# Sliding-window attention with sinks: one merged block of 128 visible logits in place of two masked blocks

## The chip, the cores and the metric

The kernel runs on one core of one Trainium2 chip. The metric is device time in microseconds, measured as the median of several executions; one further execution is recorded by the hardware profiler. Engines are named as in the profile: PE is TensorE (PEld its weight loads), DVE VectorE, ACT ScalarE, POOL GpSimd, SP the engine that issues most transfers.

## The reference, cut to what matters

Two decoder layers on 2048 tokens of width 1024, float32. Layer A (forgetting attention) and the shared keys and values are not touched. Layer B is the part in question: 16 query heads in 4 groups share 4 key/value heads of 64 columns; each query sees the 128 keys up to its own, and a learned sink per head takes part in the softmax but brings no value.

```python
logits = jnp.einsum('bnqhgd,bnkhd->bnhgqk', qb, k_band) * scale    # k_band: previous and own block of 128
diff = (jnp.arange(WINDOW)[:, None] + WINDOW) - jnp.arange(2 * WINDOW)[None, :]
in_window = (diff >= 0) & (diff < WINDOW)
...
logits = jnp.where(valid[None, :, None, None], logits, -jnp.inf)
probs = jax.nn.softmax(jnp.concatenate([logits, sink], axis=-1), axis=-1)[..., :-1]
out = jnp.einsum('bnhgqk,bnkhd->bnqhgd', probs, v_band)
...
h = h + (o * jax.nn.silu(gate)) @ w_out_b[j]
```

For query q of a block, key column j of the own block is visible if j <= q, and column j of the previous block if j > q. So exactly one of the two is visible for every j, and 128 in all.

## The kernel before, in words

The sequence is cut into 16 blocks of 128 queries. A unit is one block i and one group g of four heads: 64 units, unit u = 4 i + g. Every float32 product is made of split operands: a high part (rounded for the fast matmul) and a low part (what is left).

`attention_b` (L1239) writes its work as steps. Step n (L1423) holds, in this order:

- **scores(n)** (L1274): for each of four heads two matmuls (L1279, L1282) of 256 key columns into one PSUM tile of two banks; a masked maximum per head on VectorE (L1288), which adds the band mask in PSUM and reduces; small instructions for the negated maximum and the sink (L1294, L1297, L1298); four exponentials with row sums on ScalarE (L1301); sum and reciprocal (L1305, L1306); normalization of all 1024 columns on GpSimd (L1307).
- **weights_t(n - 3)** (L1311): eight transposes of 128 x 128 on TensorE (helper line L347) into a PSUM tile of two banks, then the high part by ScalarE (L1325) and the low part by VectorE (L1326).
- six matmuls of the output projection (L1404), fed from a generator that works eight steps behind.
- **values(n - 4)** (L1329): four matmuls of 512 columns (L1337): two blocks, each by high and low part. Both halves of the value split lie side by side, so ScalarE copies the low half of the result to SBUF (L1344), VectorE adds the halves in two instructions (L1346), GpSimd multiplies by the gate (L1350), ScalarE and VectorE split the result again (L1352, L1353).
- six more projection matmuls. Half a block's projection takes 24 of them in one PSUM bank `pb`; VectorE adds the residual (L1410) and a transfer stores it.

Block 0 has no previous block: its four units work on 128 columns. `load` (L1247) fetches queries and keys of the next block in three transfers and clears part of an operand tile on GpSimd (L1257); `load_v` fetches values and gates. In steps 4 to 11 the output weights are loaded and split (L1386 on ScalarE, L1387 on VectorE, 1024 columns each).

The first eight steps run inside `projections`: the last eight gate tiles of 24 matmuls (L720) each have one attention step ahead of them (the `hook`, L714). From step 8 on projection fills TensorE.

PSUM has eight banks; the layout `BANKS` gives `b2` three tiles of two banks, `pa` and `pb` one each. Scores and transposes draw from `b2`, values from `pa`, projection from `pb`, the gate from `pb` and `b2` in turn.

The order in which the code is written is not the order on each engine. When the program is built, a scheduler fixes the order of each engine's instructions from modelled times, and waits are set by tile; the trace shows the order that came out.

Of the kernel before, what the change touches and what calls it, by code (L numbers as in the profile page):

```python
# [13 lines left out]
F32R = mybir.dt.float32r  # L14
BF16 = mybir.dt.bfloat16
I32 = mybir.dt.int32
AF = mybir.ActivationFunctionType
# [70 lines left out]

BANKS = dict(b2=3, pa=1, pb=1)
BANKS_ATT = dict(sc=3, mx=1, pa=1, pb=1, ac=1)  # L90

# [58 lines left out]
class Trunk:  # L150
# [56 lines left out]
    def constants(self):  # L207
# [30 lines left out]

        self.band = tile_("band", [P, 2, P], BF16)
        nc.gpsimd.memset(self.band, 0.0)  # L240
        select(self.band[:, 0, :], self.band[:, 0, :], [[1, P]], -1, -1, NEG)
        select(self.band[:, 1, :], self.band[:, 1, :], [[-1, P]], 0, 1, NEG)

# [29 lines left out]
        self.gq16 = row("gq16", a["qnorm_b_g"][:, :ROT], ROT)  # L273
        self.nsink = tile_("nsink", [P, H])

# [6 lines left out]
    def vectors(self):  # L282

        nc = self.nc
        self.load_vectors(self.loads[1:])
        for t in (self.g_qb, self.g_kb):
            for s in range(2):
                nc.vector.memset(t[s * HD : s * HD + ROT, :], 1.0)
        nc.vector.tensor_single_scalar(self.nsink, self.sink, -1.0, ALU.mult)

# [331 lines left out]
    def projections(self, normed, groups, row, later=None, pre=None, hook=None, first=None):  # L622
# [75 lines left out]
        for gi, grp in enumerate(groups):  # L698
# [539 lines left out]
    def attention_b(self, w_out, res, dst):  # L1238
# [3 lines left out]
        N = len(units)  # L1242
        blk, st = {}, {}

        def load(i):

            k0 = max(i - 1, 0) * P  # L1247
            w = (i + 1) * P - k0
            ts_ = slice(i * P, (i + 1) * P)
            t = self.sb("big", [P, 4 * 1024], F32R)  # L1250
# [6 lines left out]
            nc.gpsimd.memset(f_(k2[:HD, :, :w]), 0.0)  # L1257
# [16 lines left out]
        def scores(u):  # L1274
            i, g = units[u]
            ka, k2, qa, _, _, w = blk[i]
            ps = self.ps("b2", [P, G, 2 * P])
            for h in range(G):
                nc.tensor.matmul(  # L1279
                    ps[:, h, :w], qa[:, g * G + h, :], ka[:, g, :w], start=True, stop=False  # L1280
                )
                nc.tensor.matmul(  # L1282
                    ps[:, h, :w], qa[:, g * G + h, :], k2[:, g, :w], start=False, stop=True
                )
            mx = self.sb("mx", [P, G], bufs=6)
            mask = self.band.rearrange("p b k -> p (b k)")[:, 2 * P - w :]
            for h in range(G):
                nc.vector.tensor_tensor_reduce(  # L1288
                    out=ps[:, h, :w], in0=ps[:, h, :w], in1=mask, scale=1.0, scalar=NEG,
                    op0=ALU.add, op1=ALU.max, accum_out=mx[:, h : h + 1],  # L1290
                )
            nm, es, rs = (self.sb(x, [P, G], bufs=6) for x in ("nm", "es", "rs"))
            hs = slice(g * G, (g + 1) * G)
            nc.vector.scalar_tensor_tensor(  # L1294
                nm, mx, -(HD**-0.5), self.nsink[:, hs], ALU.mult, ALU.min
            )
            nc.vector.tensor_tensor(es, nm, self.sink[:, hs], ALU.add)  # L1297
            nc.scalar.activation(es, es, AF.Exp)  # L1298
            pf = self.sb("st", [P, G, 2 * P])
            for h in range(G):  # L1300
                nc.scalar.activation(  # L1301
                    pf[:, h, :w], ps[:, h, :w], AF.Exp, bias=nm[:, h : h + 1],
                    scale=HD**-0.5, accum_out=rs[:, h : h + 1],
                )
            nc.vector.tensor_tensor(rs, rs, es, ALU.add)  # L1305
            nc.vector.reciprocal(rs, rs)  # L1306
            nc.gpsimd.tensor_tensor(  # L1307
                pf[:, :, :w], pf[:, :, :w], rs.unsqueeze(2).to_broadcast([P, G, w]), ALU.mult
            )
            st[u] = pf  # L1310

        def weights_t(u):

            i, g = units[u]
            nb = blk[i][5] // P
# [5 lines left out]
            ph, pl = (  # L1321
                php[:, 2 * k + u % 2, :].rearrange("p (b h q) -> p b h q", b=2, h=G)
                for k in range(2)
            )
            nc.scalar.copy(ph[:, :nb], ps[:, :nb])  # L1325
            nc.vector.tensor_tensor(pl[:, :nb], ps[:, :nb], f_(ph[:, :nb]), ALU.subtract)  # L1326
            st[u] = (ph, pl)

        def values(u):  # L1329
            i, g = units[u]  # L1330
            ph, pl = st.pop(u)
            nb = blk[i][5] // P
            pv = self.ps("pa", [P, G, P])
            for b in range(nb):
                v = blk[i - nb + 1 + b][3]
                for n_, src in enumerate((ph, pl)):
                    nc.tensor.matmul(  # L1337
                        pv.rearrange("p h q -> p (h q)"), v[:, g, :],
                        src[:, b].rearrange("p h q -> p (h q)"),
                        start=(b == 0 and n_ == 0), stop=(b == nb - 1 and n_ == 1),  # L1340
                    )
            t = self.sb("wr", [P, 8, P])
            cr, y = t[:HD, :G, :], t[:, G : G + G // 2, :]
            nc.scalar.copy(cr, pv[HD:])  # L1344
            for s in range(2):
                nc.vector.tensor_tensor(  # L1346
                    y[s * HD : (s + 1) * HD], pv[:HD, s::2, :], cr[:, s::2, :], ALU.add
                )
            pr = slice(g * G // 2, (g + 1) * G // 2)
            nc.gpsimd.tensor_tensor(y, y, blk[i][4][:, pr, :], ALU.mult)  # L1350
            yh, yl = (yt(i, k, pr) for k in range(2))
# [38 lines left out]
        load_v(0)  # L1390
        yield

        def project():
# [29 lines left out]
        for n in range(N + V_LAG_B):  # L1423
            if n < N:
                scores(n)
            if n == T_LAG_B:
                php = self.sb("big", [P, 4, 1024], F32R)
            if n == V_LAG_B + NKV:
# [141 lines left out]
```

## Time and profile before

| | |
|---|---|
| runs of the kernel before, us | 2503.91, 2504.49, 2506.16 (median 2504.49) |
| profiled execution, its own time, us | 2501.05 |
| its span in the profile, us | 2499.3 |
| mean granted TensorE clock | 0.998 |
| first and last score matmul of layer B, us from the span's start | 2089.8 and 2459.2 |
| first and last projection matmul (L1404) | 2150.3 and 2495.1 |

The span is cut on the page into shares by engine; since stages differ, the shares of layer B's attention are read from windows between the times in the last two rows. A row of the groups gives the line of the code, the engine, the operation, output and inputs by name, shapes and count, then busy time, mean ns of one, and how long the engine sat idle before it and for whom. A row of the timeline gives start, length, engine, line, and in brackets the idle time before it with its cause. A weight load (PEld) overlaps the matmul before it, so starts of successive weight loads show the pace of TensorE better than lengths of matmuls.

### The profile page before, as it was taken

What the parts mean: (1) busy time and instruction counts of PE and PEld (TensorE: products, weight loads), DVE (VectorE), ACT (ScalarE), POOL (GpSimd) and SP (SyncE); (2) the same over time, 40 slices, a digit from 0 to 9 for tenths busy, and PEclk for the clock granted to TensorE, in tenths of its full rate; (3) what the DMA queues carried; (4) which work ended last, traced back from release to release, by engine and by line L of the source; (5) the groups of instructions that cost most, each with busy time, mean ns of one, the idle gap of its engine ahead of it and who ended that gap; (6) DMA issues with size and microseconds to landing.
All of it is one profiled execution on the core that took longest, in us unless ns stands there. A gap on an engine that the chain in (4) does not pass through costs nothing.

```text
span 2499.3 us, 37273 instructions
## 1 busy us (share of the span) xinstructions
PE 2450.7 (98%) x12256; PEld 2048.9 (82%) x12256; DVE 1798.3 (72%) x4279; ACT 1307.5 (52%) x2553; POOL 920.6 (37%) x611
## 2 busy tenths in 40 slices
PE   8999999999999999999999999999999999899999
PEld 6788899988888887877877778888888888788887
DVE  7656667736888888888888965556666434888885
ACT  5423333414777777777777761145332213677674
POOL 0000000013777777777777752200011001355543
PEclk9999999999999999999999999999999999999999
DMA  5656545687545655565465559965443424665561
GB/s 183 201 160 190 174 147 157 192 273 220 147 144 157 192 147 157 145 198 150 131 193 166 153 168 291 287 214 165 114 127 88 128 97 143 188 170 159 160 170 64
DMA packets 351520, 419.29 MB, mean 168 GB/s; under 512 B 64928, under 2 KB 248256, under 8 KB 345152
## 3 DMA queue, kind: packets, MB, share of 16 engines
q1 hardware_dynamic: 351328, 416.92, 57.3%
q8 instruction: 97, 1.59, 0.3%
q14 instruction: 95, 0.78, 0.1%
HBM read 265.29 MB, written 151.40 MB: 167 GB/s over the span
## 4 chain that ended last, share of the span: by engine, by line
PE 48%; DVE 4%; DMA 2%; ACT 2%; issue 1%; POOL 1%; SPq 0%; POOLq 0%; ACTq 0%; DVEq 0%
PE b L757 9%; PE pb L1404 6%; PE b L1220 5%; PE pa L1025 4%; PE pb L1059 3%; PE pb L720 3%; PE b L720 3%; PE b L347 2%; PE mx L934 2%; PE sc L983 2%; PE pa L1337 2%; PE sc L982 2%; DMA wr<-wg 1%; PE b L1282 1%; PE b L1279 1%
## 5 line engine op out<-in xcount | busy, mean ns | idle before, releaser
L757 PE MATMUL b<-wh,big 128*128 128x512 f32 (+3 forms) x2560 | 769.9, 375 | 8.9 <-ACT wh L484 8.9
L1001 POOL TENSOR_TENSOR big<-st,big 128x1024 fp32r<-128x1024 f32 (+1 forms) x320 | 659.7, 2076 | 273.6 <-ACT big L1000 171.8
L757 PEld LDWEIGHTS b<-wh,big 128*128 128x128 f32 x2560 | 471.4, 188 | 79.3 <-ACT wh L484 10.9
L757 PE MATMUL b<-wl,big 128*128 128x512 f32 (+3 forms) x1280 | 473.7, 370 | 1.7 <-DVE wl L485 1.7
L1010 DVE TENSOR_TENSOR ac<-ac,st 128x512 f32<-128x512 f32 (+3 forms) x576 | 355.0, 616 | 53.2 <-ACT st L997 24.5
L997 ACT ACTIVATE st<-sc 128x512 f32<-128x512 f32 (+1 forms) x512 | 274.9, 584 | 157.6 <-PE sc L983 79.4
L1025 PE MATMUL pa<-big 128*128 128x512 f32 (+3 forms) x1280 | 327.1, 370 | 3.1 <-POOL big L1001 1.0
L1000 ACT CAST big<-st 128x1024 fp32r<-128x1024 f32 (+1 forms) x320 | 295.5, 924 | 8.0
L757 PEld LDWEIGHTS b<-wl,big 128*128 128x128 f32 x1280 | 241.4, 189 | 38.3 <-DVE wl L485 5.8
L1025 PEld LDWEIGHTS pa<-big 128*128 128x128 f32 x1280 | 222.8, 190 | 49.1 <-ACT sq L1033 16.8
L945 DVE CUSTOM_DVE_ANT_0 mx<-mx,rot 128x128 f32<-128x128 f32 (+3 forms) x240 | 210.5, 877 | 39.6 <-PE mx L934 34.5
L493 ACT ACTIVATE sq<-b,r 128x512 f32<-128x512 f32 (+2 forms) x128 | 77.8, 608 | 301.2 <-PE b L757 298.1
L982 PE MATMUL sc<-big 128*128 128x512 f32 (+3 forms) x640 | 231.1, 365 | 1.3 <-DVE st L540 1.1
L983 PE MATMUL sc<-big 67*128 67x512 f32 (+3 forms) x640 | 229.7, 368 | 0.0
L934 PE MATMUL mx<-big 66*128 66x128 f32 (+3 forms) x660 | 192.1, 365 | 10.4 <-DVE mt L945 9.8
L1059 PE MATMUL pb<-wh,wr 128*128 128x512 f32 x488 | 179.4, 399 | 3.7 <-DMA wr<-wg 3.1
L495 DVE TENSOR_REDUCE sm<-sq 128x8 f32<-128x512 f32 (+2 forms) x128 | 74.9, 585 | 138.9 <-ACT sq L493 138.7
L857 POOL MEMSET rot<- 128x1024 bf16 x1 | 1.0, 952 | 421.0 <-PE pb L347 421.0
L934 PEld LDWEIGHTS mx<-big 66*128 66x128 f32 x660 | 113.6, 191 | 50.0 <-DVE mt L945 20.2
L1307 POOL TENSOR_TENSOR st<-st,rs 128x1024 f32<-128x1024 f32 (+1 forms) x64 | 118.0, 1843 | 93.4 <-DVE rs L1306 88.1
L982 PEld LDWEIGHTS sc<-big 128*128 128x128 f32 x640 | 121.7, 190 | 23.2 <-DVE st L540 1.5
L983 PEld LDWEIGHTS sc<-big 67*128 67x128 f32 x640 | 121.7, 190 | 21.2
(258 smaller groups left out, 4349.3 us busy)
## 6 DMA issues: line engine op xcount, KB each, us to landing
wr<-wg SPq DMA_DIRECT2D x62, 512.0 KB
va<-st SPq DMA_DIRECT2D x32, 512.0 KB
ka<-st SPq DMA_DIRECT2D x64, 256.0 KB
ut<-big SPq DMA_DIRECT2D x16, 1024.0 KB
big<-ka SPq DMA_DIRECT2D x16, 1024.0 KB
big<-qa SPq DMA_DIRECT2D x16, 1024.0 KB
qb<-st SPq DMA_DIRECT2D x64, 256.0 KB
big<-qb SPq DMA_DIRECT2D x16, 1024.0 KB
```

The lines of the kernel that those rows point to most:

```text
L720: nc.tensor.matmul(ps, W[k][dt][:, ft * P : (ft + 1) * P], u[ch][:, dt, :], start=(dt == 0 and i == 0), stop=(dt == NDT - 1 and i == 2),)
L757: nc.tensor.matmul(ps[:, :n], u[tb // 4][:, dt, us], W[k][dt], start=(dt == 0 and i == 0), stop=(dt == NDT - 1 and i == 2),)
L934: mm = nc.tensor.matmul(ps[:, b, :wb], qb[:66, i * P : (i + 1) * P], kb[:66, k0 + b * wb : k0 + (b + 1) * wb], start=True, stop=True,)
L945: nc.vector.tensor_tensor_reduce(out=lg, in0=lg, in1=mask, scale=1.0, scalar=NEG, op0=ALU.add, op1=ALU.max, accum_out=f_(o),)
L982: nc.tensor.matmul(o, ka[:, ks], qa[:, qs], start=not (last and n_), stop=False)
L983: nc.tensor.matmul(o, kb[:, ks], qb[:, qs], start=False, stop=not diag)
L997: nc.scalar.activation(pf[:, off : off + w], ps[:, :w], AF.Exp, scale=HD**-0.5)
L1000: nc.scalar.copy(ph[:, :tw], pf[:, :tw])
L1001: nc.gpsimd.tensor_tensor(pl[:, :tw], pf[:, :tw], f_(ph[:, :tw]), ALU.subtract)
L1010: nc.vector.tensor_tensor(a_, a_, pf[:, off : off + w], ALU.add)
L1025: nc.tensor.matmul(pv[:, q0 : q0 + w], v[:, k, :], src[:, off : off + w], start=(p == 0 and n_ == 0 and i == 0), stop=(last and n_ == 1 an ...
L1059: nc.tensor.matmul(ps, w[:, dt // 2 % 2, wk, dt % 2, :], us[dt][uk], start=(dt == 0 and i == 0), stop=(dt == NDT - 1 and i == 2),)
```

## The change

Layer B's attention is rewritten so that each unit carries one block of 128 logits a head.

- The masks: `band[:, 0]` holds the causal mask for block 0, `band[:, 1]` is 1 where the key column is after the query. The factor 1/8 moves from the exponential into the query gain; the negated sinks and their exponential are dropped.
- **scores**: the same matmuls, placed so that own logits lie in the upper 128 columns. A predicated copy puts the previous block's logits over the hidden ones. The sink is copied into the column just ahead; one maximum over 129 columns, and four exponentials of 129 columns whose row sums hold the sink.
- **weights_t**: four transposes into a PSUM tile of one bank (`fl`), high and low part of 512 columns; then GpSimd multiplies both by the lower triangle (1024 columns).
- **differences**, new, once per block from block 1: value differences between own and previous block, split again, on GpSimd with one ScalarE copy.
- **values**: previous values by high and low part of all weights, plus differences by the triangle's part: four matmuls as before. The output stays in the PSUM tile; the gate product moves to VectorE.
- The operand tiles of `load` are two fixed ones, cleared once each. From the second hook on, the layout `BANKS_B` holds; gate tiles then take `pa` in place of `b2`.

```diff
+BANKS_B = dict(b2=2, fl=1, pa=2, pb=1)
...
+        select(self.band[:, 0, :], self.band[:, 0, :], [[-1, P]], 0, 1, NEG)
+        nc.vector.tensor_tensor(self.band[:, 1], self.tri, self.ident, ALU.subtract)
...
+        nc.vector.tensor_single_scalar(self.g_qb, self.g_qb, HD**-0.5, ALU.mult)
...
-                        ps = self.ps(("pb", "b2")[ft % 2], [P, CH])
+                        ps = self.ps(("pb", "pa" if "fl" in self.banks else "b2")[ft % 2], [P, CH])
...
-            for h in range(G):
-                nc.vector.tensor_tensor_reduce(
-                    out=ps[:, h, :w], in0=ps[:, h, :w], in1=mask, scale=1.0, scalar=NEG,
-                    op0=ALU.add, op1=ALU.max, accum_out=mx[:, h : h + 1],
-                )
...
+                m = self.band[:, 1].bitcast(I16).unsqueeze(1).to_broadcast([P, G, P])
+                nc.vector.copy_predicated(lg, m, ps[:, :, :P])
+            nc.vector.tensor_copy(ps[:, :, P - 1], self.sink[:, g * G : (g + 1) * G])
+            lg = ps[:, :, P - 1 :]
+            nm, rs = (self.sb(x, [P, G], bufs=6) for x in ("nm", "rs"))
+            nc.vector.tensor_reduce(nm, lg, AX.X, ALU.max, negate=True)
+            pf = self.sb("st", [P, G, P + 1])
...
             nc.gpsimd.tensor_tensor(
-                pf[:, :, :w], pf[:, :, :w], rs.unsqueeze(2).to_broadcast([P, G, w]), ALU.mult
+                pf, pf, rs.unsqueeze(2).to_broadcast([P, G, P]), ALU.mult
             )
...
-            ps = self.ps("b2", [P, 2, G, P])
-            for b in range(nb):
-                for h in range(G):
-                    self.flip(ps[:, b, h, :], pf[:, h, b * P : (b + 1) * P])
+            ps = self.ps("fl", [P, G, P])
+            for h in range(G):
+                self.flip(ps[:, h, :], pf[:, h])
+            both, own = (php[:, u % 2, k] for k in range(2))
+            ph, pl = (both[:, k] for k in range(2))
+            nc.scalar.copy(ph, ps)
+            nc.vector.tensor_tensor(pl, ps, f_(ph), ALU.subtract)
+            if i:
+                tri = self.tri.unsqueeze(1).to_broadcast([P, 2 * G, P])
+                nc.gpsimd.tensor_tensor(
+                    own.rearrange("p k h q -> p (k h) q"),
+                    f_(both).rearrange("p k h q -> p (k h) q"), tri, ALU.mult,
+                )
...
+        def differences(i):
+            v, before = f_(blk[i][3]), f_(blk[i - 1][3])
+            t = self.sb("wl", [P, NKV, P])
+            nc.gpsimd.tensor_tensor(t, v, before, ALU.subtract)
+            t_ = t[:, :, :HD]
+            nc.gpsimd.tensor_tensor(t_, t_, t[:, :, HD:], ALU.add)
+            dv = self.sb("wh", [P, NKV, P], F32R)
+            nc.scalar.copy(dv[:, :, :HD], t_)
+            nc.gpsimd.tensor_tensor(dv[:, :, HD:], t_, f_(dv[:, :, :HD]), ALU.subtract)
+            dvs[i] = dv
...
+                terms = ((v, ph), (v, pl), (dv, oh), (dv, ol))
...
+            y = pv[:, 1::2, :]
+            for s in (1, 0):
...
-            nc.gpsimd.tensor_tensor(y, y, blk[i][4][:, pr, :], ALU.mult)
+            nc.vector.tensor_tensor(y, y, blk[i][4][:, pr, :], ALU.mult)
...
+            if n % NKV == 1 and NKV < n < N:
+                differences(n // NKV)
```

More of the change, by code (lines that the diff above doesn't have):

```diff
@@ L1249, in load @@
             ts_ = slice(i * P, (i + 1) * P)
-            t = self.sb("big", [P, 4 * 1024], F32R)
+            if i < 2:
+                operands[i] = self.sb("big", [P, 4 * 1024], F32R)
+            t = operands[i % 2]
             qa = t[:, : H * P].rearrange("p (h q) -> p h q", q=P)
@@ L1292, in scores @@
[L1292 to L1299, printed above, removed]
+                for j, k in enumerate((ka, k2)):
+                    nc.tensor.matmul(
+                        ps[:, h, 2 * P - w :], qa[:, g * G + h, :], k[:, g, :w],
+                        start=j == 0, stop=j == 1,
+                    )
@@ new lines, in weights_t @@
+            st[u] = (ph, pl, own[:, 0], own[:, 1])
+        def differences(i):
[8 more added lines that the diff above has]
+            dvs[i] = dv
@@ L1342, in values @@
-            t = self.sb("wr", [P, 8, P])
-            cr, y = t[:HD, :G, :], t[:, G : G + G // 2, :]
+            ph, pl, oh, ol = st.pop(u)
+            if i:
+                v, dv = blk[i - 1][3], dvs[i]
+                terms = ((v, ph), (v, pl), (dv, oh), (dv, ol))
+            else:
+                v = blk[i][3]
+                terms = ((v, ph), (v, pl))
+            pv = self.ps("pa", [P, G, P])
+            for n_, (v, src) in enumerate(terms):
+                nc.tensor.matmul(
+                    pv.rearrange("p h q -> p (h q)"), v[:, g, :],
+                    src.rearrange("p h q -> p (h q)"),
+                    start=n_ == 0, stop=n_ == len(terms) - 1,
+                )
@@ L1426, in attention_b @@
             if n == T_LAG_B:
[L1427 removed]
+                php = self.sb("big", [P, 2, 2, 2, G, P], F32R)
             if n == V_LAG_B + NKV:
```

53 lines of the change are left out of this document (16 added, 37 removed).

## The prediction

> **What bounds the kernel now.** I read the page's busy times first, then the stretches of the timeline by windows to find the stage, then one step of it instruction by instruction.
>
> ```profile
> span 2499.3 us, 37273 instructions
> PE 2450.7 (98%) x12256; PEld 2048.9 (82%) x12256; DVE 1798.3 (72%) x4279; ACT 1307.5 (52%) x2553; POOL 920.6 (37%) x611
> ```
> ```profile
> core 0: us, PE busy (x) PEld busy (x) DVE busy (x) ACT busy (x) POOL busy (x), PEclk, DMA share, GB/s
> 2125.00:2135.00 10.00, 8.16 (x43) 6.82 (x42) 8.53 (x24) 5.50 (x16) 2.64 (x3) 1.00 0.65 183
> 2145.00:2155.00 10.00, 9.13 (x52) 7.73 (x50) 8.93 (x23) 5.31 (x14) 2.64 (x2) 1.00 0.55 165
> 2165.00:2175.00 10.00, 5.78 (x32) 4.38 (x30) 8.71 (x26) 7.12 (x23) 4.26 (x4) 1.00 0.89 262
> 2250.00:2300.00 50.00, 50.00 (x293) 43.76 (x292) 44.48 (x152) 35.78 (x111) 25.62 (x21) 1.00 0.56 155
> ```
>
> In the settled part of layer B's attention (2250 to 2300) TensorE is never idle and its clock is full; VectorE is at 89%, ScalarE at 72%, GpSimd at 51%. Before that, while the output weights are being split, TensorE loses 1.84, 0.87 and 4.22 us in three stretches. A busy row alone doesn't prove a bound, so here is one step, the weight loads of TensorE in order:
>
> ```profile
> 2300.05 1.23 PEld L1404 LDWEIGHTS pb<-big 128*128 128x128 f32 x6
> 2301.32 0.88 PEld L1337 LDWEIGHTS pa<-big,qn 128*128 128x128 f32 x4
> 2302.24 1.32 PEld L1404 LDWEIGHTS pb<-big 128*128 128x128 f32 x6
> 2303.61 0.19 PEld L1279 LDWEIGHTS b<-big 128*128 128x128 f32 x1
> 2304.68 0.90 PEld L347 LDWEIGHTS b<-ident,st 128*128 128x128 f32 x8
> 2305.55 1.22 PEld L1404 LDWEIGHTS pb<-big 128*128 128x128 f32 x6
> ```
>
> Start to start: six projection matmuls 1.27 us (P), four value matmuls 0.92 (V), six more 1.37 (P), eight score matmuls 1.07 (S), eight transposes 0.87 (F); the step is 5.50 us and nothing in it waits. A transpose thus costs 0.87 / 8 = 0.109 us of TensorE's own time. What TensorE issues per unit sets the period.
>
> **The change part by part.** Durations for the other engines come from these groups (window from 2000 to 2500, shapes apart; the last line from the page):
>
> ```profile
> L1288 DVE CUSTOM_DVE_ANT_0 b<-b,band 128x256 f32<-128x256 f32 x240 | 102.0, 425 | 21.3 <-PE b L1282 16.7
> L1288 DVE DVE_READ_ACCUMULATOR2_ANT mx<- 128x1 f32 x256 | 34.4, 134 | 0.6
> L1297 DVE TENSOR_TENSOR es<-nm,sink 128x4 f32<-128x4 f32 x64 | 10.8, 169 | 2.1
> L1325 ACT CAST big<-b 128x512 fp32r<-128x512 f32 x4 | 2.4, 588 | 0.0
> L1326 DVE TENSOR_TENSOR big<-b,big 128x1024 fp32r<-128x1024 f32 x60 | 73.2, 1220 | 2.2 <-ACT big L1325 2.1
> L1326 DVE TENSOR_TENSOR big<-b,big 128x512 fp32r<-128x512 f32 x4 | 2.7, 682 | 0.0
> L1346 DVE TENSOR_TENSOR wr<-pa,wr 64x256 f32<-64x256 f32 x128 | 52.9, 414 | 3.1 <-ACT wr L1344 2.0
> L1353 DVE TENSOR_TENSOR big<-wr,big 128x256 fp32r<-128x256 f32 x32 | 13.6, 426 | 4.6 <-ACT big L1352 1.6
> L1387 DVE TENSOR_TENSOR big<-wr,big 128x1024 fp32r<-128x1024 f32 x8 | 16.0, 1998 | 0.0
> L1410 DVE TENSOR_TENSOR sq<-pb,sq 128x512 f32<-128x512 f32 x32 | 22.1, 691 | 12.8 <-PE pb L1404 11.9
> L1307 POOL TENSOR_TENSOR st<-st,rs 128x1024 f32<-128x1024 f32 x60 | 113.8, 1897 | 70.9 <-DVE rs L1306 65.6 <-DVE nm L1294 3.8 <-DVE mx L1288 1.6
> L1307 POOL TENSOR_TENSOR st<-st,rs 128x512 f32<-128x512 f32 x4 | 4.2, 1041 | 22.5 <-DVE rs L1306 22.5
> L1350 POOL TENSOR_TENSOR wr<-wr,big 128x256 f32<-128x256 f32 x64 | 48.1, 752 | 119.4 <-DVE wr L1346 94.4 <-issue 25.1
> L1001 POOL TENSOR_TENSOR big<-st,big 128x1024 fp32r<-128x1024 f32 (+1 forms) x320 | 659.7, 2076 | 273.6 <-ACT big L1000 171.8
> ```
>
> **TensorE.** Scores keep eight matmuls. Values keep four: two blocks by high and low part become previous values and differences by high and low part. Projection is untouched. Only the transposes change: a unit of blocks 1 to 15 turns one merged 128-column block a head, so four transposes and not eight. 60 units x 4 x 0.109 = 26.1 us, all on the path that sets the end; the period becomes 5.50 - 0.44 = 5.06 us. The first four units had four transposes already.
>
> **VectorE, per unit.** Before, as sums of durations: four masked maxima 4 x (0.425 + 0.134) = 2.24, four small ones (L1294, L1297, L1305, L1306) at L1297's 0.169 = 0.68, low part 1.22, two additions 0.83, low part of the output 0.43, half a residual addition 0.35: 5.75. The trace shows 44.48 / 50 x 5.50 = 4.89 busy per unit, because successive instructions overlap a little: a factor of 0.85. After: one predicated copy, one sink column 0.17, one maximum over 4 x 129, one reciprocal 0.17, low part 0.68, additions 0.83, the gate product that comes over from GpSimd 0.43, output low part 0.43, residual 0.35. No predicated copy is in the trace. The nearest row with two inputs, one in PSUM, and 512 elements is L1410, 0.691 us; the low end is L1288 (0.425 for 256 elements), the high end L1326's 1.22, a second pass. I take 0.69, since it is the same size, and 0.69 for the maximum too. Sum 4.44, by the factor 3.8 us of 5.06; with 1.22 for the copy 4.2. VectorE stays under the period at either end.
>
> **ScalarE** does four exponentials of 129 and not 256 columns, no sink exponential, a 512-column copy in place of 1024, and one 256-column copy for every four units. All of it shrinks, from 72%; it costs nothing while TensorE is the bound, and if that cover went it would still be a gain.
>
> **GpSimd** is the one engine with more to do: normalizing falls from 1.90 to 1.04, the gate product (0.75) leaves, the product with the triangle comes (1024 elements: 1.90 by L1307, 2.08 by L1001, whose output type it shares, so 2.08), and three difference steps per block (1.04 + 2 x 0.75) / 4 = 0.64. Sum 3.8 us of 5.06. As throughput this is hidden behind TensorE. As latency it stands on a new path: transposes, high part, low part, triangle product, then V one step later. From the end of F to that V lie P, V, P, S, F, P = 1.27 + 0.92 + 1.37 + 1.07 + 0.44 + 1.27 = 6.34 us; the path needs 0.59 (L1325) + 0.68 + 2.08 = 3.35 plus queues. I cost it at nothing; the cover is 3.0 us, and each further microsecond of queue would be lost once per unit, 60 us in all.
>
> **Weight splitting (units 8 to 11).** There VectorE needs 4.89 + 2.00 (L1387) per 5.50 us step and TensorE waits for it, in all 1.84 + 0.87 + 4.22 = 6.9 us. After, it needs 3.8 + 2.0 per 5.06: the excess falls from 1.4 to 0.7 us per step, so half the loss goes, 3.5 us; bounds 0 to 6.9. L1387's own length comes from a collision, seen in these two rows:
>
> ```profile
> 2172.00 1.89 POOL L1307 TENSOR_TENSOR st<-st,rs 128x1024 f32<-128x1024 f32 x1 [1.87 <-DVE nm L1294]
> 2172.13 2.84 DVE L1387 TENSOR_TENSOR big<-wr,big 128x1024 fp32r<-128x1024 f32 x1
> ```
>
> It ends 1.08 us after GpSimd's product, as if it had begun only then. The Trainium skill, SBUF — State Buffer, section "Who interferes with whom", has the rule: a VectorE instruction with two SBUF inputs contends with a GpSimd instruction that reads SBUF, and whichever issues first holds the shared port to its end. By that rule the longer GpSimd work speaks against the change: all eight splits could stand behind a 2.08 us product, 8 x (1.08 + 2.08) - 16.0 = 9.3 us more VectorE time in this stretch and a sum some 5 us worse. In the settled part the rule finds nothing to act on, because the gate product and the output's low part then take one operand from PSUM.
>
> **Projection hand-over.** There is one projection bank, so after each half block the next P waits for the residual addition. What covers it shrinks. The tail, where F alone stands between, shows what the hand-over needs:
>
> ```profile
> 2463.90 1.04 PE L347 MATMUL b<-ident,st 128*128 128x128 f32 x8
> 2465.02 1.22 PEld L1404 LDWEIGHTS pb<-big 128*128 128x128 f32 x6 [0.33 <-DVE sq L1410]
> ```
>
> With 0.87 of cover it is 0.33 late, so it needs 1.20. Settled cover falls from S + F = 1.94 to 1.07 + 0.44 = 1.51, still enough: nothing. In the tail three hand-overs lose 0.44 of cover each: +1.3 us.
>
> **The rest** costs nothing: masks and gains are set up once, the operand tiles are double buffered as before, and 14 GpSimd clears fall away. Taking the gate's second bank from "pa" once the layout changes could hold the first scores for one gate evaluation; bounds 0 to 2.5 us, value 0.
>
> **Sum**: -26.1 - 3.5 + 1.3 = -28.3. On the profiled execution's 2501.05 us (span 2499.3 and 1.75 around it) that is 2472.8; the median of the runs, 2504.49, lies 3.4 us above that execution, so I forecast 2476 us.
>
> **Rivals.** First, the same gain, partly given back at the hand-over. These rows show what stands ahead of the residual addition:
>
> ```profile
> 2253.90 0.84 DVE L1346 TENSOR_TENSOR wr<-pa,wr 64x256 f32<-64x256 f32 x2
> 2254.77 0.69 DVE L1410 TENSOR_TENSOR sq<-pb,sq 128x512 f32<-128x512 f32 x1
> 2255.87 1.23 PEld L1404 LDWEIGHTS pb<-big 128*128 128x128 f32 x6
> ```
>
> The two output additions run first, the residual addition ends at 2255.46 and P starts 0.41 later. With 0.44 less cover that is the edge. If the output additions begin only when the last P has landed (1.20 - 0.69 = 0.51 after the cover begins), the bank is free after 0.51 + 0.84 + 0.69 = 2.04 against 1.51: 0.53 x 28 hand-overs = 15 us, 2491; with another 0.27 us of small instructions ahead, 2498. For it: this hand-over has no slack left. Against: VectorE has less to do, so its output additions should end before the last P lands, as they nearly do here (2254.74).
>
> Second, slower: GpSimd takes its work in program order, normalizing unit n ahead of the triangle product of unit n - 3, and V waits. Rows for the length of that loop:
>
> ```profile
> 2093.70 0.37 ACT L1301 ACTIVATE st<-b,nm 128x128 f32<-128x128 f32 x1 [2.40 <-DVE nm L1294]
> 2095.84 1.04 POOL L1307 TENSOR_TENSOR st<-st,rs 128x512 f32<-128x512 f32 x1 [5.06 <-DVE rs L1306]
> ```
> ```profile
> 2248.62 0.28 PE L1279 MATMUL b<-big 128*128 128x256 f32 x1
> 2249.77 0.43 DVE L1288 CUSTOM_DVE_ANT_0 b<-b,band 128x256 f32<-128x256 f32 x1 [0.51 <-PE b L1282]
> 2254.89 0.74 POOL L1350 TENSOR_TENSOR wr<-wr,big 128x256 f32<-128x256 f32 x1 [1.61 <-DVE wr L1346]
> 2256.86 1.90 POOL L1307 TENSOR_TENSOR st<-st,rs 128x1024 f32<-128x1024 f32 x1 [1.24 <-DVE rs L1306]
> ```
>
> Let x be the time from the first score matmul to normalizing: 2256.86 - 2248.62 = 8.24 now. Unobstructed after the change: 1.15 to VectorE's start, copy, sink and maximum 1.55, and 2.14 from the first 128-column exponential to normalizing: 4.84. Two steps must then hold x + 1.04 + 2.08 + V 0.92 + P 1.37, so the period is (x + 5.41) / 2. It decides from x = 4.7; at 5.6 the old period is back (about 2503, no change); halfway between the bounds, 6.5, it is 5.96, 54 us over the forecast: 2530. Against: the build does not keep program order on GpSimd. At 2254.89 the gate product of unit n - 4, written later in the step, stands ahead of normalizing unit n at 2256.86, because it is ready sooner; the triangle product would be ready sooner too.
>
> **How the numbers follow.** Forecast (2476) 0.62; hand-over 0.18; GpSimd order with a short x, no change, 0.07; the same, slower, 0.13. Low end: all 6.9 us of the splitting loss gone, no loss in the tail, transposes read as 0.90 / 8 (27.0 us), and 3.4 us for the distance between the profiled execution and the median: 2504.5 - 27.0 - 6.9 - 3.4 = 2467. High end 2498, where the hand-over case ends; the two GpSimd cases, 0.20, are left out. What a measurement can tell from no change is about 0.2%, 5 us: faster is 0.80, same 0.07, slower 0.13.
>
> **What would show it.** the transposes of attention weights fall from 60 x 8 + 4 x 4 = 496 to 64 x 4 = 256, with four value matmuls per unit as before; steps of 5.06 us and a full PE row in the settled part; a predicated copy near 0.69; PE's loss between 2125 and 2175 halved. Wrong would be: PE waiting for the triangle product ahead of V, for the residual addition ahead of P, or VectorE at 95% and more.

## The result and the profile after

The kernel after takes 2484.99 us (median of 4 runs, 2481.19 to 2486.35) against 2504.2 us for the kernel before on the same chip (4 runs, 2503.26 to 2506.16): a ratio of 0.9925 [0.9913, 0.9937], 19 us less. The forecast was 28 us less. The profiled execution took 2481.19 us. The transposes of attention weights came out as counted, 256 of them, so the question is where the missing 9 us are.

The page of the kernel after:

```profile
span 2479.5 us, 36156 instructions
PE 2428.4 (98%) x12016; PEld 2024.6 (82%) x12016; DVE 1740.5 (70%) x3832; ACT 1257.0 (51%) x2504; POOL 993.2 (40%) x637
```

The same stretches by windows, for the kernel after:

```profile
2125.00:2135.00 10.00, 10.00 (x51) 8.45 (x51) 8.72 (x17) 7.04 (x23) 1.04 (x1) 1.00 0.31 106
2145.00:2155.00 10.00, 10.00 (x58) 8.66 (x57) 7.57 (x15) 5.46 (x16) 3.68 (x3) 1.00 0.80 249
2165.00:2175.00 10.00, 9.88 (x54) 8.01 (x53) 9.31 (x22) 5.79 (x22) 9.22 (x6) 1.00 0.92 268
2250.00:2300.00 50.00, 48.13 (x263) 41.23 (x262) 37.05 (x90) 28.18 (x102) 37.10 (x25) 1.00 0.59 185
```

The three stretches in which TensorE stood waiting are full or nearly so. But the settled stretch, which was full before (50.00), now has a hole: 48.13. Every other engine has fallen except GpSimd, which rose from 25.62 to 37.10. VectorE is at 37.05 / 50 = 74%, where the forecast had 3.8 / 5.06 = 75%. None of them is short of time, so the hole must be a matter of order. The waits of TensorE's weight loads (2080 to 2500) name it; first the kernel before:

```profile
PEld pb L1404 <- DVE sq L1410: 3.8, 5, 1.4
PEld pb L1404 <- DVE big L1387: 2.7, 1, 2.7
```

and the kernel after (L1430 is the projection, L1436 the residual addition):

```profile
PEld pb L1430 <- DVE sq L1436: 18.6, 17, 1.5
PEld fl L349 <- DVE big L1327: 1.2, 1, 1.2
```

The wait of the projection for the residual addition, which frees the one projection bank, grew from 3.8 to 18.6 us. In the settled part it recurs once per block of four units, about 1.2 us each time; in the hand-overs between, there is none. "Once per block" is the clue: only one thing in the new kernel happens once per block, the value differences.

One such hand-over in the timeline of the kernel after (start, duration, engine, line; in brackets the idle time before it and its releaser):

```profile
2302.42 1.30 POOL L1340 TENSOR_TENSOR wl<-qn,rows 128x512 f32<-128x512 f32 x1
2303.80 0.73 POOL L1342 TENSOR_TENSOR wl<-wl 128x256 f32<-128x256 f32 x1
2304.56 0.41 ACT L1344 CAST wh<-wl 128x256 fp32r<-128x256 f32 x1 [1.60 <-POOL wl L1342]
2304.87 0.37 ACT L1377 CAST big<-pa 128x256 fp32r<-128x256 f32 x1
2305.28 0.42 DVE L1378 TENSOR_TENSOR big<-pa,big 128x256 fp32r<-128x256 f32 x1 [1.48 <-ACT big L1377]
2306.44 0.68 DVE L1302 TENSOR_REDUCE nm<-b 128x4 f32<-128x516 f32 x1
2306.78 1.13 PEld L1286 LDWEIGHTS b<-big 128*128 128x128 f32 x8
2307.16 0.37 ACT L1305 ACTIVATE st<-b,nm 128x129 f32<-128x129 f32 x1 [1.43 <-DVE nm L1302]
2308.70 0.18 DVE L1309 RECIPROCAL rs<-rs 128x4 f32<-128x4 f32 x1 [1.58 <-ACT st L1305]
2308.81 0.69 DVE L1436 TENSOR_TENSOR sq<-pb,sq 128x512 f32<-128x512 f32 x1
2309.56 0.30 PEld L1430 LDWEIGHTS pb<-big,wh 128*128 128x128 f32 x2 [1.24 <-DVE sq L1436]
```

Read it as a relay. GpSimd subtracts two blocks of values and joins the halves. ScalarE is to copy the high part of that, waits 1.60 us for it, and behind its copy stands the high part of the attention output (L1377), whose input has been there since 2302.81, when VectorE's gate product (L1375) ended. VectorE waits 1.48 for that, and behind its low part (L1378) stands the maximum of the next unit (L1302). ScalarE's exponentials wait 1.43 for the maximum, VectorE's reciprocal (L1309) 1.58 for the exponentials, and the residual addition is queued behind the reciprocal. Its own input, the projection, has been there since 2307.16. TensorE gets the bank 1.24 us late. An engine that is 56% busy (ScalarE, 28.18 of 50) delayed the bound, by standing still at the head of its queue.

The other terms can be read from groups of the kernel after (2000 to 2500, shapes apart; busy, mean ns of one, idle before):

```profile
L1330 POOL TENSOR_TENSOR big<-big,tri 128x1024 fp32r<-128x1024 f32 x60 | 143.9, 2399 | 68.2 <-DVE big L1327 61.6 <-DVE b L1299 4.7 <-DVE rs L1309 1.8
L1302 DVE TENSOR_REDUCE nm<-b 128x4 f32<-128x516 f32 x64 | 43.6, 682 | 0.2
L1298 DVE COPY_PREDICATED b<-band,b 128x512 f32<-128x512 int16 x60 | 41.4, 690 | 1.6 <-PE b L1286 0.8
L1412 DVE TENSOR_TENSOR big<-wr,big 128x1024 fp32r<-128x1024 f32 x8 | 10.1, 1261 | 2.5 <-ACT big L1411 2.5
L1340 POOL TENSOR_TENSOR wl<-qn 128x512 f32<-128x512 f32 x5 | 6.4, 1289 | 82.1 <-PE b L722 82.1
```

The predicated copy takes 0.690 us and the maximum 0.682, as taken in the forecast (0.69 each). The triangle product takes 2.40 us and not 2.08, the difference's first step 1.29 and not 1.04.

### The profile page after: what moved, and what is told of

The parts are those of the page before. It is cut to its first block, busy times and chain, and to the rows that moved or that the text cites. A ratio compares the mean times of both kernels' runs of the same rounds, so it can differ in the third digit from the quotient of the medians.

```text
span 2479.5 us, 36156 instructions
## 1 busy us (share of the span) xinstructions
PE 2428.4 (98%) x12016; PEld 2024.6 (82%) x12016; DVE 1740.5 (70%) x3832; ACT 1257.0 (51%) x2504; POOL 993.2 (40%) x637
## 4 chain that ended last, share of the span: by engine, by line
PE 43%; DVE 5%; ACT 3%; POOL 3%; DMA 2%; issue 2%; SPq 0%; DVEq 0%; ACTq 0%; POOLq 0%
PE b L759 10%; PE b L1222 5%; PE pa L1027 4%; PE pb L722 3%; PE pb L1061 3%; PE pb L1430 3%; PE b L722 3%; PE mx L936 2%; PE sc L985 2%; PE sc L984 2%; ACT st L1305 1%; POOL big L1330 1%; DVE big L1327 1%; PE pa L1222 1%; PE pb L1222 1%
## 5 line engine op out<-in xcount | busy, mean ns | idle before, releaser
L1330 POOL TENSOR_TENSOR big<-big,tri 128x1024 fp32r<-128x1024 f32 x60 | 143.9, 2399 | 68.2 <-DVE big L1327 61.6
```

## The experiments

**Theory A**: the missing gain is the wait of ScalarE's copy in the differences, handed on as above. **Rival B**, the prediction's own first rival: the hand-over is short at every half block, with the output additions ahead of the residual addition, so only another bank helps. **Rival C**: GpSimd, with its new triangle product, is late. **Rival D**: the transposes saved less than 26 us, because TensorE was not the only bound.

**e1: the copy goes to GpSimd**, which has just produced its input, so no other engine waits for it.

```diff
-            nc.scalar.copy(dv[:, :, :HD], t_)
+            nc.gpsimd.tensor_copy(dv[:, :, :HD], t_)
```

> The high part of the value differences is copied by GpSimd in place of ScalarE; all else as in the changed kernel. Theory A (the copy): once a block ScalarE stands 1.6 us in front of this copy because GpSimd has not finished the difference; exponentials, reciprocal and residual addition slip, and the next projection matmul waits 1.2 us, about 14 times. Then the wait of L1430 for the residual addition falls from 18.6 us to under 6 us and the time from 2485 to about 2470 us. Theory B (the cover): scores and four transposes, 1.51 us, are too short for the residual addition whatever ScalarE does. Then the wait stays at 15 to 20 us and the time within 4 us of 2485.

Measured: 2466.59 us against 2502.45 before, 0.9857 [0.9842, 0.9871]. The wait and the settled stretch of this kernel:

```profile
PEld pb L1430 <- DVE sq L1436: 4.5, 5, 1.6
```
```profile
2250.00:2300.00 50.00, 50.00 (x279) 43.32 (x278) 39.26 (x95) 29.44 (x110) 41.62 (x31) 1.00 0.57 179
```

and the same place in its block:

```profile
2294.41 0.37 ACT L1377 CAST big<-pa 128x256 fp32r<-128x256 f32 x1
2295.27 0.42 DVE L1378 TENSOR_TENSOR big<-pa,big 128x256 fp32r<-128x256 f32 x1
2296.13 0.40 POOL L1344 CAST wh<-wl 128x256 fp32r<-128x256 f32 x1
2297.10 0.37 ACT L1305 ACTIVATE st<-b,nm 128x129 f32<-128x129 f32 x1 [1.36 <-DVE nm L1302]
2298.37 1.13 PEld L1286 LDWEIGHTS b<-big 128*128 128x128 f32 x8
2298.64 0.18 DVE L1309 RECIPROCAL rs<-rs 128x4 f32<-128x4 f32 x1 [1.57 <-ACT st L1305]
2298.79 0.69 DVE L1436 TENSOR_TENSOR sq<-pb,sq 128x512 f32<-128x512 f32 x1
2299.87 0.30 PEld L1430 LDWEIGHTS pb<-big,wh 128*128 128x128 f32 x2
```

The copy still happens late (2296.13), but only GpSimd's own work, which has time, queues behind it; the output's high part on ScalarE runs at 2294.41, ahead of the score weights and not behind the copy. The residual addition starts 2298.79 - 2298.37 = 0.42 us after the score weights begin to load; in the kernel after it was 2308.81 - 2306.78 = 2.03, so 1.61 later. The bank is free at 2299.48 here, 0.39 ahead of its need: 1.61 - 0.39 = 1.22, which is the 1.24 that TensorE waited. The exponentials and the reciprocal wait in e1 too (1.36 and 1.57), so those two waits alone show no lateness. What shows it is the place of each link against the score weights: from the output's low part (L1378) to the residual addition, each starts 1.60 to 1.65 us earlier in e1. One line, and TensorE's row is full again with GpSimd busier than before (41.62). If GpSimd's work were late (rival C), this edit, which gives it more, should have made things worse. Rival B falls as well: there is still one projection bank, and of the five waits left none lies in the settled part (one comes while the weights are split, four in the tail).

**e2: no differences at all.**

```diff
-                v, dv = blk[i - 1][3], dvs[i]
+                v, dv = blk[i - 1][3], blk[i][3]
...
-            if n % NKV == 1 and NKV < n < N:
-                differences(n // NKV)
```

> The value differences are left out altogether; the values of the own block are used in their place, so the output is another one, with the same matmuls. Theory A (the copy holds up ScalarE once a block): the wait for the residual addition falls under 6 us and the time to about 2467 us, a little below the kernel with the copy on GpSimd, because GpSimd also loses 2.8 us of work per block. Theory B (the cover is too short): the wait stays at 15 to 20 us, time within 4 us of 2485.

Measured: 2468.91 us, 0.9863 [0.9846, 0.9879]; the projection waits 4.1 us for the residual addition. The same as e1: in e1 the differences cost nothing that can be measured, and in the kernel after they cost what e1 wins back.

**e3: the differences written one step later**.

```diff
-            if n % NKV == 1 and NKV < n < N:
+            if n % NKV == 2 and NKV < n < N:
```

> The differences are written one step later in each block (steps with n % 4 = 2 in place of 1), so that no hand-over of the projection bank follows at the end of that step; the copy stays on ScalarE. Theory A: ScalarE still waits about 1.6 us for GpSimd, but what slips is a step without hand-over; the wait for the residual addition falls to about half, time 2472 to 2479 us. Theory B: no difference, within 4 us of 2485.

Measured: 2483.13 us, 0.9924 [0.9909, 0.9939]; no change, a miss. The trace of e3 shows why it tells nothing on theory A:

```profile
2302.52 1.28 POOL L1340 TENSOR_TENSOR wl<-qn,rows 128x512 f32<-128x512 f32 x1
2304.65 0.41 ACT L1344 CAST wh<-wl 128x256 fp32r<-128x256 f32 x1 [1.63 <-POOL wl L1342]
```

The chain runs at the place where it ran before (2302.42 and 2304.56). The build orders each engine's work by when it reckons it ready, so a line moved in the source need not move on the engine. The trace, not the source, says whether an edit took place.

**e4: the kernel before, with only one of its two blocks of weights transposed and split**: the transposes' saving, with the copy and the low part of 512 columns in place of 1024 that go with it, and nothing else of the change.

```diff
-            for b in range(nb):
-                for h in range(G):
-                    self.flip(ps[:, b, h, :], pf[:, h, b * P : (b + 1) * P])
+            for h in range(G):
+                self.flip(ps[:, 0, h, :], pf[:, h, :P])
...
-            nc.scalar.copy(ph[:, :nb], ps[:, :nb])
+            nc.scalar.copy(ph[:, :1], ps[:, :1])
...
```

> The kernel before, but with the weights of the first of its two blocks alone transposed and split (four transposes in place of eight, 512 and not 1024 columns of high and low part), and used for both blocks, so the output is another one; the four value matmuls stay. TensorE theory of the prediction: 60 x 4 x 0.109 = 26 us less, and some of the 6.9 us lost in the splitting stretch, so about 2474 to 2477 us, steps of 5.06 us. Theory A says the same, since there are no differences in it. Theory B: hand-overs late by up to 0.5 us each, 2480 to 2490 us.

Measured: 2476.37 us (2474.48 to 2483.27) against 2502.45: 26.1 us less by the medians, and by the ratio, 0.9901 [0.9884, 0.9917], 24.8, give or take 4. The forecast was 26.1. Rival D falls, from the side of the kernel before.

**e6: e1 with each transpose of the blocks 1 to 15 done twice**, the same price from the other side.

```diff
-                self.flip(ps[:, h, :], pf[:, h])
+                for _ in range(2 if i else 1):
+                    self.flip(ps[:, h, :], pf[:, h])
```

> The kernel with the copy on GpSimd (2466.6 us), in which each unit of blocks 1 to 15 makes its four transposes twice, into the same place. If TensorE's own issue is now the bound: 60 x 4 x 0.109 = 26 us more, 2490 to 2495 us, and steps of 5.50 us. If the hand-over or another engine is the bound, the added cover is partly free: under 2485 us.

Measured: 2494.48 us against 2505.04, 0.9963 [0.995, 0.9976]; e1 stands at 0.9857, so the 240 transposes cost 0.0106 x 2505 = 26.5 us, give or take 5. In e1 TensorE is the bound, and it pays in full for each transpose.

**e7: e1 without the triangle product.**

```diff
-            if i:
-                tri = self.tri.unsqueeze(1).to_broadcast([P, 2 * G, P])
-                nc.gpsimd.tensor_tensor(
...
-            st[u] = (ph, pl, own[:, 0], own[:, 1])
+            st[u] = (ph, pl, ph, pl)
```

> The kernel with the copy on GpSimd (2466.6 us), with the product with the triangle left out (the differences are multiplied by all weights, so the output is another one). The prediction costed that product at nothing, behind TensorE: then within 4 us of 2466.6 although GpSimd loses 2.4 us per unit. The prediction's second rival (values wait for it): 10 us or more less, 2457 us or below.

Measured: 2467.74 us, 0.9853 [0.9835, 0.9872]; no change against e1's 0.9857. GpSimd falls from 41.62 to 18.09 of 50 in the settled stretch, and nothing gets faster: 2.40 us per unit are wholly hidden. Rival C is out, and with it the prediction's second rival.

**e5: the residual addition ahead of the reciprocal** (ScalarE's copy stays where it was). It cuts the last link of the relay and not the first.

```diff
-            nc.vector.reciprocal(rs, rs)
...
+        def normalize(u):
+            pf, rs = st[u]
+            if adds:
+                with self.tc.issue_after(adds.pop()):
+                    nc.vector.reciprocal(rs, rs)
...
+            if 0 <= n - 1 < N:
+                normalize(n - 1)
```

> The changed kernel with the copy of the differences left on ScalarE, but on VectorE the residual addition is put ahead of the reciprocal at each hand-over (reciprocal and normalization are written one step later and queued behind the addition). ScalarE should still wait some 22 us in all for GpSimd. Theory A2 (the lateness reaches TensorE by one link only: exponentials, then the reciprocal at the head of VectorE's queue, then the residual addition behind it): the wait for the residual addition falls from 18.6 us under 6 us, time 2467 to 2473 us. Rival (ScalarE's lateness reaches TensorE also by the high part of the weights or the output, or slows every engine alike): time stays above 2479 us.

Measured: 2477.15 us, 0.9895 [0.988, 0.991]: about half of what was expected. The wait in the trace of e5, in all and at one place:

```profile
PEld pb L1438 <- DVE sq L1444: 13.4, 17, 1.6
```
```profile
2264.36 0.30 PEld L1438 LDWEIGHTS pb<-big,wh 128*128 128x128 f32 x2 [0.78 <-DVE sq L1444]
```

So the expectation was half wrong: the reciprocal accounts for some 0.4 us of each 1.2. The rest comes earlier. The output's low part waits for ScalarE, and the low part of the weights and the maximum, which stand behind it on VectorE, reach the residual addition that much later.

**e8: e1 and e5 together.**

> Both mends together: the copy on GpSimd, and the residual addition ahead of the reciprocal. If one lateness was the whole of the settled loss, either mend alone takes it away and both bring no more than 3 us beyond the better one: 2463 to 2467 us. If they were two separate losses they would add up: about 2455 us.

Measured: 2466.28 us, 0.985 [0.9835, 0.9864], the same as e1. The two edits repair one lateness and not two. In e8 the wait has turned round:

```profile
DVE sq L1444 <- PE pb L1438: 54.9, 28, 5.9
```
```profile
2296.96 0.69 DVE L1444 TENSOR_TENSOR sq<-pb,sq 128x512 f32<-128x512 f32 x1 [1.69 <-PE pb L1438]
2298.05 0.30 PEld L1438 LDWEIGHTS pb<-big,wh 128*128 128x128 f32 x2
```

VectorE now waits for TensorE, 28 times in 32. The bank comes free no earlier for that: at this hand-over the residual addition ends at 2297.65, 0.40 us ahead of need, against 0.39 in e1, because it can't begin before the projection has landed. What e8 adds is 1.7 us for which VectorE has nothing to do at a hand-over. It brings no more time, as TensorE was full already. e1 and e8 are the fastest versions here (e2 and e7 are about as fast, but leave out part of the work), 36 to 38 us under the kernel before and about 18 under the kernel after.

**e9 and e10: two projection banks and one value bank**, on the kernel after (e9) and on e1 (e10). Rival B asks for that bank.

```diff
-BANKS_B = dict(b2=2, fl=1, pa=2, pb=1)
+BANKS_B = dict(b2=2, fl=1, pa=1, pb=2)
```

> The changed kernel, copy still on ScalarE, with two banks for projection and one for values in place of one and two. If ScalarE's lateness costs TensorE time at the hand-over of the projection bank and nowhere else, a second bank hides it: the wait for the residual addition falls from 18.6 us under 3 us and the time to 2464 to 2472 us. If the single value bank, which the outputs now occupy from the value matmuls to the output's low part, is late for the next unit, value matmuls wait instead and the time stays at 2480 us or rises.

> The same two projection banks and one value bank, with the copy on GpSimd. The lateness is gone anyway; the second bank can only take the 4.5 us that hand-overs still cost in the tail and at the start: 2461 to 2466 us. If the single value bank is late: 2470 us or more, with value matmuls waiting.

Measured: e9 2493.84 us, 0.9961 [0.9946, 0.9976], and e10 2482.97, 0.9921 [0.9906, 0.9935], both against 2502.72. The projection no longer waits for the residual addition, as asked, and both are slower than with the bank as it was: by about 9 us (0.9961 against 0.9925) and 16 us (0.9921 against 0.9857). The waits of e10, of weight loads and of VectorE:

```profile
PEld fl L349 <- DVE big L1327: 10.1, 31, 0.6
PEld pb L1430 <- ACT wh L1377: 4.4, 12, 0.8
```
```profile
DVE big L1327 <- PE pa L1361: 31.0, 31, 1.3
```

The transposes now wait for the low part of the weights, and that waits for value matmuls: it is written into one of two buffers (`php[:, u % 2]`), which the value matmuls of two units before read. The orders on TensorE and on VectorE have changed along with the bank. How much of the 16 us is the missing value bank and how much those orders wasn't separated.

**e12: e1 with the attention output in SBUF**, where the gate product stays on VectorE; the change keeps it in PSUM.

```diff
-            cr = self.sb("wr", [HD, G, P])
+            t = self.sb("wr", [P, 8, P])
+            cr = t[:HD, :G, :]
...
-            y = pv[:, 1::2, :]
+            y = t[:, G : G + G // 2, :]
```

> The kernel with the copy on GpSimd, outputs added into SBUF in place of PSUM, but the gate product left on VectorE. VectorE is at 78% there and TensorE the bound: within 4 us of 2466.6. By the rule that a VectorE instruction with two SBUF inputs contends with GpSimd's reads, gate product and low part would now queue behind GpSimd's products of 1.0 to 2.4 us: then VectorE is late at hand-overs and the time is 2475 us or more. The price of that rule is worked out from this kernel's own rows.

Measured: 2489.08 us, 0.9949 [0.9932, 0.9966]; against e1's 0.9857 that is 23 us more. The same two products, first in the kernel after:

```profile
L1375 DVE TENSOR_TENSOR pa<-pa,big 128x256 f32<-128x256 f32 x64 | 27.1, 423 | 1.1
L1378 DVE TENSOR_TENSOR big<-pa,big 128x256 fp32r<-128x256 f32 x32 | 13.2, 412 | 8.6 <-ACT big L1377 8.6
```

and in e12, with both inputs in SBUF:

```profile
L1376 DVE TENSOR_TENSOR wr<-wr,big 128x256 f32<-128x256 f32 x64 | 49.7, 777 | 1.0
L1379 DVE TENSOR_TENSOR big<-wr,big 128x256 fp32r<-128x256 f32 x32 | 24.0, 749 | 1.8 <-ACT big L1378 1.8
```

The size is the same and the mean goes from 0.42 to 0.76 us. It is not that SBUF is slower in itself: the shortest of the 64 gate products takes 0.38 us in e12 and 0.40 in the kernel after, but the longest 2.62 against 0.43. **e11** does the same and puts the gate product back on GpSimd.

```diff
-            nc.vector.tensor_tensor(y, y, blk[i][4][:, pr, :], ALU.mult)
+            nc.gpsimd.tensor_tensor(y, y, blk[i][4][:, pr, :], ALU.mult)
```

> The kernel with the copy on GpSimd, with the outputs' place undone: they are added into SBUF and multiplied by the gate on GpSimd, as in the kernel before. GpSimd is at 83% in the settled part; 0.75 us per step of 5.06 us brings it to 98%. If TensorE still is the only bound: within 4 us of 2466.6. If GpSimd becomes the bound, value matmuls wait for the triangle product: 2472 to 2490 us.

Measured: 2570.55 us, 1.027 [1.0255, 1.0285], 100 us more than e1 and far beyond what was expected. Two rows of its timeline and its settled stretch:

```profile
2301.95 2.38 POOL L1330 TENSOR_TENSOR big<-big,tri 128x1024 fp32r<-128x1024 f32 x1 [0.46 <-DVE big L1327]
2301.96 2.66 DVE L1379 TENSOR_TENSOR big<-wr,big 128x256 fp32r<-128x256 f32 x1
```
```profile
2250.00:2300.00 50.00, 40.76 (x213) 34.06 (x211) 35.10 (x62) 23.36 (x87) 36.39 (x31) 0.96 0.45 137
```

GpSimd is no fuller than in the kernel after (36.39 against 37.10): it wasn't overloaded. A VectorE instruction of 0.42 us is held for 2.66, from 0.01 us after GpSimd's product began until 0.29 after it ended. That is the rule which the prediction weighed, from the Trainium skill, SBUF — State Buffer, section "Who interferes with whom": two SBUF inputs on VectorE against a GpSimd instruction that reads SBUF, and the first one keeps the port. The trace agrees, but for the 0.29 us after the product's end, a little less than the whole instruction takes. Besides, the output's way now leads from VectorE to GpSimd to ScalarE and back to VectorE, and TensorE's clock was granted at 0.96. TensorE's weight loads wait 51.2 us for the residual addition and 24.8 for the low part of the weights, in e1 4.5 and 0.2 (2080 to 2560); so some 71 of the 100 us are added waits of these two kinds. How the 100 us divide between holding, the longer way and the clock wasn't separated.

## Why the prediction was right and wrong

**Transposes, -26.1: right.** e4 gave 26.1 by the medians, e6 26.5, each within 4 to 5 us. In the kernel after the score weights load at 2301.72 and 2306.78: a step of 5.06 us, the figure forecast, wherever nothing waits.

**Predicated copy, maximum, VectorE's share: right** (0.690, 0.682, and 74%, or 79% in e1, where TensorE is full). **GpSimd hidden as throughput: right** (e7), though the triangle product was mis-sized, 2.40 for 2.08. The row chosen, L1001, was of the right kind, with two operands of full width and the same output type, but it was read off the page, where its 2.08 is a mean over three shapes ("+1 forms"). With shapes apart, the kernel before already has the size that came:

```profile
L1001 POOL TENSOR_TENSOR big<-st,big 128x1024 fp32r<-128x1024 f32 x192 | 461.5, 2412 | 142.8 <-ACT big L1000 77.7 <-PE sc L983 50.0 <-PE pb L1059 10.5
```

The first step of the differences was read off L1307, where the second operand is one number per head: that takes 1.04 for 512 elements, two full operands 1.29 (L1340). Between 512 and 1024 full elements lie 2.40 - 1.29 = 1.11 us, 2.17 ns for each. The Trainium skill, GPSIMD Engine Reference, section "Elementwise — side-by-side cycle accounting", puts an instruction on two tensors at about 2.6 cycles an element, with 1.2 GHz; the estimate from that is 2.17 ns, and the trace agrees.

**The step that failed** is "Projection hand-over": "Settled cover falls from S + F = 1.94 to 1.07 + 0.44 = 1.51, still enough: nothing". The cover was right: 1.51 against a need of 1.20 leaves 0.31, and e1 shows 0.39 to spare. What was not looked at is what could make the residual addition late by more than that. The differences' copy had been priced on ScalarE as busy time ("All of it shrinks, from 72%; it costs nothing while TensorE is the bound"), and by busy time it is nothing, 0.41 us in every four units. Its price is what it waits for: 1.60 us at the head of ScalarE's queue, with the output's high part behind it. The prediction followed the queue on GpSimd for the triangle product, and not the one on ScalarE for this copy. Between 2190 and 2417 twelve such waits add up to 14.2 us; the profiled executions of the kernel after and of e1 differ by 15.5, and the runs by 0.0068 x 2502 = 17, give or take 5.

The **first rival** (2491) had the place and the symptom, and nearly the size (15 us against 14 to 17). That the size came so near is luck: it has other instructions ahead of the residual addition, and 0.53 us at each of 28 hand-overs in place of 1.2 at every second one, 12 in all. A second bank, its natural remedy, made things worse when it was taken from the values (e9).

**Splitting weights, -3.5 (bounds 0 to 6.9)**: the term was too small. The forecast took all of TensorE's idle time in this stretch for the splitting's. By the same measure, between 2085 and 2205, it is 7.6 us before, 4.1 after and 1.7 in e1, so 5.9 us are won here once the hand-over is mended. How much of that is the splitting's own isn't shown: the waits before name the low part of a split (L1387) once, with 2.7 us. The excess per step was worked out from 2.00 us for L1387, of which part was its collision with GpSimd. Most of that collision went: the eight take 1.26 us each (L1412), 10.1 us together against 16.0, and two of them, of 1.30 and 1.49 us, begin during a GpSimd product, in its last half microsecond. The rule of the Trainium skill, which was weighed against the change at this place with 5 us, found the other six out of GpSimd's way.

**The tail, +1.3**: the sign was wrong. From the last score matmul to the end of the span it is 40.1 us before, 37.5 after and 37.4 in e1. Four units of transposes are left there, 1.7 us of the difference. The waits for the residual addition went from 3.2 us to 3.0, so the hand-overs lost nothing; the rest of the gain, some 0.6 us, wasn't traced. The forecast had three hand-overs covered by transposes alone. In the kernel before there are two (0.33 and 0.31 us late), and two with no transposes ahead of them at all (1.39 and 1.21). In the kernel after a pair of value matmuls comes between:

```profile
2446.05 0.59 PEld L349 LDWEIGHTS fl<-ident,st 128*128 128x128 f32 x4
2446.61 0.30 PEld L1361 LDWEIGHTS pa<-big,rows 128*128 128x128 f32 x2
2447.22 1.23 PEld L1430 LDWEIGHTS pb<-big 128*128 128x128 f32 x6 [0.31 <-DVE sq L1436]
```

The sum for e1, in which the hand-over is mended: transposes -26.1, the splitting stretch -5.9, tail -1.0, and -1.5 for an earlier start of the first scores (2089.8 to 2088.3), which the forecast had at 0; together -34.5; the profiled executions, 2501.05 and 2465.64, differ by 35.4. In the kernel after 15 us of this are lost again between first and last score (353.0 us against 338.0 in e1, from 369.4 before). So the 9 us between forecast and result are what is left of two errors of opposite sign, 15 us lost at the hand-over and some 6 won beyond the forecast in the last three terms. That the time came so near is partly luck.

**Outputs kept in PSUM, at nothing**: the prediction said that the rule of the Trainium skill finds nothing to act on in the settled part, because the gate product and the output's low part take one operand from PSUM. That held (0.42 and 0.41 us), but what it saves was not priced. e12 shows the price: with both operands in SBUF the kernel loses 23 us, nearly as much as the transposes win. The second value bank may be worth up to 16 us (e10, where the orders changed with it).

## What to carry to other kernels

Price an added instruction twice: by its duration, and by how long it will stand at the head of its engine's in-order queue waiting for its input; then follow who is queued behind it until you reach the bound. Where an engine's queue leads to the bound, try giving a short step of a chain to the engine that makes its input. And when a row stands for several shapes, take the shapes apart before using its mean. An engine's busy share did not show the loss: ScalarE was 56% busy, and 1.61 us of lateness met a hand-over with 0.39 us to spare.

## What was not expected of the hardware

- A 0.42 us VectorE instruction took 2.66 us when it met a GpSimd product of 2.38 us with both its inputs in SBUF (e11); with one input in PSUM the same work stays at 0.40 to 0.43 beside GpSimd products that fill 74% of the time.
- The hold goes both ways: in the kernel after a weight split (L1412) runs from 2165.03 to 2166.52, and the normalizing product that GpSimd begins at 2165.41 takes 2.02 us in place of 1.04, about the 1.11 us longer that the split still ran.
- A predicated copy costs what an addition of the same size costs: 0.690 us against 0.689 for L1436, both 128x512 with one operand in PSUM.
- In e11 TensorE's granted clock was 0.86 to 0.96 in each of the seven stretches of 50 us from 2150 to 2500, where no single wait of its weight loads was longer than 2.6 us. Why wasn't tested.
